# The moving inputs of the products with stationary weights begin 448 bytes past a multiple of 512, the weights' parts on one

## The chip, the cores and the metric

The kernel runs on one core of a Trainium2 chip, in one launch. The metric is the device time of that launch in microseconds (us). The engines are TensorE (PE in the rows, its weight loads PEld), VectorE (DVE), ScalarE (ACT), GpSimd (POOL) and SyncE (SP, which here issues the loads of the weights).

## The reference

Two layers of a streaming encoder on 256 tokens of width 2048, all in float32. Layer 0 mixes tokens by differential attention, layer 1 by an RWKV-7 recurrence; a squared-ReLU MLP of width 8192 follows each.

```python
def sqrelu_mlp(h, w1, w2):
    u = jax.nn.relu(h @ w1)
    return (u * u) @ w2

def reference(x, ...):
    for i in range(DEPTH):            # 2
        hn = rms_norm(x, g_pre_mix[i])
        if i % N_MIXERS == 0:
            m = diff_attention(hn, da_wq[j], da_wk[j], da_wv[j], da_wo[j], ...)
        else:
            m = rwkv7_time_mix(hn, rw_mix[j], rw_wr[j], rw_wk[j], rw_wv[j], rw_wo[j], ...)
        x = x + rms_norm(m, g_post_mix[i])
        hn = rms_norm(x, g_pre_ffn[i])
        x = x + rms_norm(sqrelu_mlp(hn, ffn_w1[i], ffn_w2[i]), g_post_ffn[i])
    return x
```

## The kernel before

Every large product is made of three products in the type float32r: each float32 operand is split in two parts, hi and lo, and hi x hi, lo x hi and hi x lo are added up in PSUM. The weights come from HBM in units of 1 MB (128 partitions x 2048 numbers), as two raw tiles of 512 KB each, issued on SyncE's queue (`raw`, L109). `parts` (L104) splits a raw tile: ScalarE casts it to `whi` (L106), VectorE subtracts to get `wlo` (L107). There are four buffers each of `raw`, `whi` and `wlo`, so two units of each; the next unit is fetched while the one before is multiplied.

There are two forms of the product. In `mm_b` (L217, with `mm_bh`, L225) the weights are stationary: a 128 x 128 block of `whi` or `wlo` is loaded into the array and 256 columns (all tokens) of the input move past it. A unit is 48 such matmuls, 2 column blocks x 8 chunks of the contraction x 3:

```python
            xh, xl = XH[c][:, k, :], XL[c][:, k, :]
            nc.tensor.matmul(ps[m], lhsT=wh[:, k, cl], rhs=xh, start=first and k == 0, stop=False)
            nc.tensor.matmul(ps[m], lhsT=wh[:, k, cl], rhs=xl, start=False, stop=False)
            e = nc.tensor.matmul(ps[m], lhsT=wl[:, k, cl], rhs=xh, start=False, stop=last and k == 3)
```

It serves the query and key projections, the first product of both MLPs, and the r and k projections of RWKV. In `mm_a` (L199) it is the other way round: 128 tokens of the input are stationary and 512 columns of the weights move, 24 matmuls to a unit. It serves the value and output projections and the second product of the MLPs. Plain float32 products, not split, are in the attention scores, in the LoRA panels of RWKV (L752) and in its scan.

The inputs of `mm_b` are the tiles `xh`, `xl` of attention (L404, L405), `fxh`, `fxl` of the MLPs (L577, L578), each 4 chunks x 256 tokens, 4,096 bytes per partition, and `mh`, `ml` of RWKV (L735), of the same size, from a pool that is opened behind the constants' tile `rcst` (L698) and the tiles R. ScalarE and VectorE write them (`gained`, L274, and `split`, L690).

By the sizes of what is allocated ahead of them, all of these begin on a multiple of 512 bytes in each partition: `whi` at 35,328 = 69 x 512 and three times 4,096 above, `wlo` at 51,712 = 101 x 512 and above, `xh0` at 110,592 = 216 x 512, `fxh0` at 107,520 = 210 x 512, the first of `mh` at 98,816 = 193 x 512. A chunk of an input is 1,024 bytes and a block of weights 512, so every operand of every float32r product begins on a multiple of 512.

The order of the work is the program's on each engine. `proj_b` (L236) goes through panels of 256 outputs, two units each, and evacuates PSUM behind each panel; side jobs (`beside`, `tick`) are put between half units, in RWKV above all.

Of the kernel before, what the change touches and what calls it, by code (L numbers as in the profile page):

```python
# [10 lines left out]
F32 = mybir.dt.float32  # L11
F32R = mybir.dt.float32r
# [7 lines left out]
S = 256  # L20
P = 128
# [13 lines left out]
class Kern:  # L35
# [38 lines left out]

    def ps(self, role):
        return self.pp.tile([P, 512], F32, name="ps_" + role, tag=role, bufs=self.roles[role])

    def small(self, n, name):
        return self.sm.tile([P, n], F32, name=name, tag="sm", bufs=48)
# [118 lines left out]

    def mm_a(self, ps, XH, XL, unit, kt0, first, last, ts=range(2), x=slice(0, 512)):  # L199

        nc = self.nc
        for t in ts:
            for half in range(2):
                wh, wl = (w.rearrange("p (k c) -> p k c", k=2)[:, :, x] for w in unit[half])
                for k in range(2):
                    kt = kt0 + half * 2 + k
                    xh = XH[kt // 4][:, kt % 4, t * P:(t + 1) * P]
                    xl = XL[kt // 4][:, kt % 4, t * P:(t + 1) * P]
                    st = first and half == 0 and k == 0
                    sp = last and half == 1 and k == 1  # L210
                    nc.tensor.matmul(ps[t][:, x], lhsT=xh, rhs=wh[:, k, :], start=st, stop=False)  # L211
                    nc.tensor.matmul(ps[t][:, x], lhsT=xh, rhs=wl[:, k, :], start=False, stop=False)  # L212
                    e = nc.tensor.matmul(ps[t][:, x], lhsT=xl, rhs=wh[:, k, :], start=False, stop=sp)  # L213
                self.tick()
        return e

    def mm_b(self, ps, XH, XL, unit, kt0, first, last):  # L217

        for m in range(2):
            for half in range(2):  # L220
                e = self.mm_bh(ps, XH, XL, unit[half], kt0 // 4 + half, m, first and half == 0, last and half == 1)
                self.tick()
        return e

    def mm_bh(self, ps, XH, XL, half, c, m, first, last, ks=range(4)):  # L225
        nc = self.nc
        wh, wl = (w.rearrange("p (k c) -> p k c", k=4) for w in half)
        cl = slice(m * P, (m + 1) * P)
        for k in ks:
# [4 lines that stand above are left out]
        return e  # L234
# [153 lines left out]
    def attention(self, xs):  # L388
        nc, a, tc = self.nc, self.a, self.tc
        with ExitStack() as ctx:  # L390
# [3 lines left out]
            xhl = ctx.enter_context(tc.tile_pool(name="at_x", bufs=1))  # L394
# [3 lines left out]
            XH, XL = [], []  # L398
# [2 lines left out]
            ps0 = [pb[:, S * m:S * m + S] for m in range(2)]  # L401
            loads = []
            for c in range(4):
                XH.append(xhl.tile([P, 4, S], F32R, name=f"xh{c}"))  # L404
                XL.append(xhl.tile([P, 4, S], F32R, name=f"xl{c}"))  # L405
                raw = self.wp.tile([P, 1024], F32, name="raw", tag="raw", bufs=RAW)
                for k in range(0, 4, 2):
                    x = slice(k * 256, (k + 2) * 256)
                    nc.sync.dma_start(raw[:, x], a["wq"][0, c // 2][:, 1024 * (c % 2):1024 * (c % 2) + 1024][:, x])
                    nc.sync.dma_start(xt[c][:, k:k + 2, :], a["xT"][c][:, k:k + 2, :])  # L410
                loads.append(raw)
# [9 lines left out]
            cst = ac.tile([P, 768], F32, name="cst")  # L421
# [147 lines left out]
    def ffn(self, i, xs, fin, store=None):  # L569
# [3 lines left out]
        with ExitStack() as ctx:  # L573
            pool = ctx.enter_context(tc.tile_pool(name=f"ff{i}", bufs=8))
            tmp = ctx.enter_context(tc.tile_pool(name=f"ff{i}_t", bufs=2))
            xhl = ctx.enter_context(tc.tile_pool(name=f"ff{i}_x", bufs=1))
            XH = [xhl.tile([P, 4, S], F32R, name=f"fxh{c}") for c in range(4)]  # L577
            XL = [xhl.tile([P, 4, S], F32R, name=f"fxl{c}") for c in range(4)]  # L578
            gf = self.vec[f"gf{i}"]

            ps0 = [self.ps(r)[:, :S] for r in ("mm", "mm", "a", "a")]
# [88 lines left out]
    def rwkv(self, xs, fin, xctx, pctx):  # L670
        nc, a, tc = self.nc, self.a, self.tc
        outer = ExitStack()
        pool = outer.enter_context(tc.tile_pool(name="rw", bufs=1))
# [21 lines left out]
        with ExitStack() as kc:  # L695
            rp = kc.enter_context(tc.tile_pool(name="rr", bufs=1))

            cst = rp.tile([P, 896], F32, name="rcst")  # L698
            nc.gpsimd.dma_start(cst[:, :776], a["c_rw"][:, P:])
            self.restart = cst[:, 0:512]  # L700
            self.ind = cst[:, 512:520].rearrange("p (i h) -> p i h", i=2)
# [4 lines left out]
            with ExitStack() as ctx:  # L706
# [81 lines left out]
                for c in range(4):  # L788
# [3 lines left out]
                    for k0 in range(0, 4, step):  # L792
# [9 lines left out]
                        f = nc.scalar.copy(MH[c][:, kk, :], m[:, kk, :])  # L802
# [692 lines left out]
```

## Time and profile before

| | |
|---|---|
| median of 3 runs | 2516.78 us (2514.69 to 2521.74) |
| the profiled execution | 2519.97 us, span 2518.2 us |
| PE busy | 2468.2 us, 98% |
| PE weight loads busy | 2245.1 us, 89% |
| VectorE busy | 1596.0 us, 63% |
| ScalarE busy | 1161.5 us, 46% |
| GpSimd busy | 207.2 us, 8% |
| HBM read and written | 433.99 and 15.20 MB, 178 GB/s over the span |
| mean granted TensorE clock | 0.992 of full speed |

A matmul's busy time runs from its start to a modelled end and overlaps the next one's, so how fast PE goes is read from the distances between starts. PEld is the loading of stationary blocks, which runs beside the matmuls.

### The profile page before, as it was taken

The page shows a single profiled execution, that of the slowest core. Times are in us where ns is not written, and L with a number is a line of the kernel's source. Part 1 is how long each engine was busy: PE and PEld are TensorE (multiplying, and loading weights), DVE is VectorE, ACT ScalarE, POOL GpSimd, SP SyncE. Part 2 cuts the span into 40 slices and gives each one's busy share as a digit, 9 for nine tenths or more (in the row PEclk, how much of TensorE's full clock was granted, in tenths as well). Part 3 has the DMA queues.
Part 4 walks back from the last instruction along what each step waited for, and adds up shares of the span by engine and source line. Part 5 has one row for each costly group of instructions (what it writes and reads, how often), then busy time and mean ns, then how long its engine had stood idle before and what let it go on. Part 6 is the DMA issues. An engine that isn't in the chain of part 4 may idle for free.

```text
span 2518.2 us, 42348 instructions
## 1 busy us (share of the span) xinstructions
PE 2468.2 (98%) x17128; PEld 2245.1 (89%) x17128; DVE 1596.0 (63%) x2498; ACT 1161.5 (46%) x1669; POOL 207.2 (8%) x234
## 2 busy tenths in 40 slices
PE   8999999999999999997999999999999999999997
PEld 8998889989989989986899988888998998998986
DVE  6667978645655556669578865557864555654655
ACT  5435645444434434455555543444544444443443
POOL 1000000000000000014301252211000000000001
PEclk9999999999999999998999999999999999999999
DMA  8655455555555555553456764334555555555554
GB/s 279 200 188 178 150 168 170 186 196 186 184 195 188 186 190 185 189 183 124 157 171 217 250 197 129 99 93 165 173 186 191 187 186 193 184 186 195 186 190 138
DMA packets 140852, 453.01 MB, mean 180 GB/s; under 512 B 27536, under 2 KB 27792, under 8 KB 140656
## 3 DMA queue, kind: packets, MB, share of 16 engines
q1 hardware_dynamic: 120176, 424.46, 51.3%
q0 software_dynamic: 5568, 16.52, 1.8%
q10 hardware_dynamic: 14912, 9.32, 1.2%
q8 instruction: 134, 2.20, 0.4%
q14 instruction: 62, 0.51, 0.1%
HBM read 433.99 MB, written 15.20 MB: 178 GB/s over the span
## 4 chain that ended last, share of the span: by engine, by line
PE 93%; DVE 4%; issue 1%; ACT 1%; POOL 0%; DMA 0%; SPq 0%; DVEq 0%; ACTq 0%
PE ps_mm L231 8%; PE ps_mm L232 8%; PE ps_mm L233 8%; PE ps_mm L211 7%; PE ps_mm L213 7%; PE ps_mm L212 7%; PE ps_a L211 7%; PE ps_a L233 6%; PE ps_a L232 6%; PE ps_a L231 6%; PE ps_a L212 6%; PE ps_a L213 6%; PE ps_c L1165 1%; DVE wlo L107 1%; PE ps_mm L1250 1%
## 5 line engine op out<-in xcount | busy, mean ns | idle before, releaser
L107 DVE TENSOR_TENSOR wlo<-raw,whi 128x1024 fp32r<-128x1024 f32 (+1 forms) x766 | 937.8, 1228 | 632.6 <-ACT whi L106 617.6
L106 ACT CAST whi<-raw 128x1024 fp32r<-128x1024 f32 (+1 forms) x776 | 809.0, 1046 | 703.2 <-PE ps_mm L213 221.3
L231 PE MATMUL ps_mm<-fxh,whi 128*128 128x256 f32 x1024 | 290.2, 284 | 0.0
L232 PE MATMUL ps_mm<-fxl,whi 128*128 128x256 f32 x1024 | 290.0, 283 | 0.0
L231 PE MATMUL ps_a<-fxh,whi 128*128 128x256 f32 x1024 | 289.8, 283 | 0.0
L232 PE MATMUL ps_a<-fxl,whi 128*128 128x256 f32 x1024 | 289.8, 283 | 0.0
L233 PE MATMUL ps_a<-fxh,wlo 128*128 128x256 f32 x1024 | 289.8, 283 | 0.0
L233 PE MATMUL ps_mm<-fxh,wlo 128*128 128x256 f32 x1024 | 289.7, 283 | 0.0
L211 PE MATMUL ps_mm<-whi,uh 128*128 128x512 f32 (+1 forms) x544 | 208.3, 383 | 0.0
L212 PE MATMUL ps_mm<-wlo,uh 128*128 128x512 f32 (+1 forms) x544 | 208.3, 383 | 0.0
L213 PE MATMUL ps_mm<-whi,ul 128*128 128x512 f32 (+1 forms) x544 | 208.2, 383 | 0.0
L232 PEld LDWEIGHTS ps_mm<-fxl,whi 128*128 128x128 f32 x1024 | 196.5, 192 | 0.3
L231 PEld LDWEIGHTS ps_a<-fxh,whi 128*128 128x128 f32 x1024 | 196.6, 192 | 0.0
L232 PEld LDWEIGHTS ps_a<-fxl,whi 128*128 128x128 f32 x1024 | 196.6, 192 | 0.0
L233 PEld LDWEIGHTS ps_a<-fxh,wlo 128*128 128x128 f32 x1024 | 196.6, 192 | 0.0
L231 PEld LDWEIGHTS ps_mm<-fxh,whi 128*128 128x128 f32 x1024 | 196.3, 192 | 0.3
L233 PEld LDWEIGHTS ps_mm<-fxh,wlo 128*128 128x128 f32 x1024 | 196.5, 192 | 0.0
L212 PE MATMUL ps_a<-wlo,uh 128*128 128x512 f32 (+1 forms) x512 | 196.0, 383 | 0.0
L213 PE MATMUL ps_a<-whi,ul 128*128 128x512 f32 (+1 forms) x512 | 195.7, 382 | 0.0
L211 PE MATMUL ps_a<-whi,uh 128*128 128x512 f32 (+1 forms) x512 | 195.5, 382 | 0.0
L628 ACT CAST uh<-r 128x256 fp32r<-128x256 f32 x128 | 51.8, 406 | 272.7 <-DVE r L627 272.7
L232 PE MATMUL ps_mm<-ml,whi 128*128 128x256 f32 x416 | 119.5, 288 | 6.5 <-DVE ml L803 6.5
(404 smaller groups left out, 4816.5 us busy)
## 6 DMA issues: line engine op xcount, KB each, us to landing
raw<-in_ffn SPq DMA_DIRECT2D x512, 512.0 KB, 4.3
raw<-in_wk SPq DMA_DIRECT2D x32, 512.0 KB, 4.3
raw<-in_wv SPq DMA_DIRECT2D x32, 512.0 KB, 4.3
raw<-in_wo SPq DMA_DIRECT2D x32, 512.0 KB, 4.2
raw<-in_rwr SPq DMA_DIRECT2D x32, 512.0 KB, 4.6
raw<-in_rwk SPq DMA_DIRECT2D x32, 512.0 KB, 4.3
raw<-in_rwv SPq DMA_DIRECT2D x32, 512.0 KB, 4.9
raw<-in_rwo SPq DMA_DIRECT2D x32, 512.0 KB, 4.2
```

The lines of the kernel that those rows point to most:

```text
L106: self.nc.scalar.copy(hi[:, x], src[:, x])
L107: (eng or self.nc.vector).tensor_tensor(lo[:, x], src[:, x], hi[:, x].bitcast(F32), op=ALU.subtract)
L211: nc.tensor.matmul(ps[t][:, x], lhsT=xh, rhs=wh[:, k, :], start=st, stop=False)
L212: nc.tensor.matmul(ps[t][:, x], lhsT=xh, rhs=wl[:, k, :], start=False, stop=False)
L213: e = nc.tensor.matmul(ps[t][:, x], lhsT=xl, rhs=wh[:, k, :], start=False, stop=sp)
L231: nc.tensor.matmul(ps[m], lhsT=wh[:, k, cl], rhs=xh, start=first and k == 0, stop=False)
L232: nc.tensor.matmul(ps[m], lhsT=wh[:, k, cl], rhs=xl, start=False, stop=False)
L233: e = nc.tensor.matmul(ps[m], lhsT=wl[:, k, cl], rhs=xh, start=False, stop=last and k == 3)
L628: nc.scalar.copy(UH[-1][:, m % 4, :], r)
L1165: nc.tensor.matmul(ps[:, c, :], lhsT=KB[q][x, i, c, :], rhs=AR[q][x, i, c].rearrange("p s t -> p (s t)"), start=True, stop=True)
L1250: nc.tensor.matmul(wps[c][:, h * 64:(h + 1) * 64], lhsT=QT[h][bK(c):bK(c) + 64, c, 0:64], rhs=VU[bK(c):bK(c) + 64, c, h * 64:(h + 1) * 64] ...
```

## The change

A helper makes a tile of 1,152 numbers instead of 1,024 and hands out the 1,024 that begin 448 bytes in. The input tiles of attention and of the MLPs come from it. In RWKV the constants' tile is made 64 bytes shorter (880 numbers instead of 896), and everything that is allocated behind it on that side begins 64 bytes lower, which is 448 past a multiple of 512: the tiles `hw`, `ha`, R, the pool with `mh` and `ml`, and the work tiles of the scan operands. The weights' parts stay where they were, and so do the inputs of the value and output projections of RWKV, those of attention's output projection, and those of the second product of the MLPs. The value projection of attention uses `xh` and `xl` too, as stationary blocks.

The padding keeps each tile's size a multiple of 512 (4,608 bytes), so `fxh1` begins 4,608 behind `fxh0`, and what comes behind the padded tiles stays on a multiple of 512.

```diff
+    def shifted(self, pool, name, o=448):
+
+        t = pool.tile([P, 1024 + 128], F32R, name=name)
+        return t[:, o // 4:o // 4 + 1024].rearrange("p (k t) -> p k t", k=4)
...
-                XH.append(xhl.tile([P, 4, S], F32R, name=f"xh{c}"))
-                XL.append(xhl.tile([P, 4, S], F32R, name=f"xl{c}"))
+                XH.append(self.shifted(xhl, f"xh{c}"))
+                XL.append(self.shifted(xhl, f"xl{c}"))
...
-            XH = [xhl.tile([P, 4, S], F32R, name=f"fxh{c}") for c in range(4)]
-            XL = [xhl.tile([P, 4, S], F32R, name=f"fxl{c}") for c in range(4)]
+            XH, XL = ([self.shifted(xhl, f"fx{y}{c}") for c in range(4)] for y in "hl")
...
-            cst = rp.tile([P, 896], F32, name="rcst")
+            cst = rp.tile([P, 880], F32, name="rcst")
```

## Rows read from the trace of the kernel before

**Rows 1.** The page: busy us, share of the span; the chain that ended last.
```profile
PE 2468.2 (98%) x17128; PEld 2245.1 (89%) x17128; DVE 1596.0 (63%) x2498; ACT 1161.5 (46%) x1669; POOL 207.2 (8%) x234
...
PE 93%; DVE 4%; issue 1%; ACT 1%; POOL 0%; DMA 0%; SPq 0%; DVEq 0%; ACTq 0%
```

**Rows 2.** Matmuls of line L231: duration ns min/median/max, first and last start.
```profile
L231 PE MATMUL ps_mm<-fxh,whi x1024: 277/283/366, 406.4 to 2403.7; 128*128 128x256 f32 x171
L231 PE MATMUL ps_a<-fxh,whi x1024: 283/283/283, 419.9 to 2415.2; 128*128 128x256 f32 x171
L231 PE MATMUL ps_mm<-mh,whi x416: 274/283/467, 1150.3 to 1420.3; 128*128 128x256 f32 x139
L231 PE MATMUL ps_mm<-xh,whi x256: 279/283/584, 6.5 to 183.6; 128*128 128x256 f32 x128
L231 PE MATMUL ps_a<-xh,whi x256: 279/283/388, 21.1 to 195.1; 128*128 128x256 f32 x128
L231 PE MATMUL ps_a<-mh,whi x96: 278/283/468, 1216.2 to 1291.6; 128*128 128x256 f32 x96
```

**Rows 3.** Timeline, first product of the MLP: start us, us, what.
```profile
600.11 0.28 PE L231 MATMUL ps_a<-fxh,whi 128*128 128x256 f32 x1
600.11 0.19 PEld L232 LDWEIGHTS ps_a<-fxl,whi 128*128 128x128 f32 x1
...
601.19 0.28 PE L231 MATMUL ps_a<-fxh,whi 128*128 128x256 f32 x1
```

**Rows 4.** Stretches: PE, PEld, DVE, ACT, POOL busy (count), clock, DMA share, GB/s.
```profile
21.00:195.00 174.00, 173.47 (x1442) 172.86 (x1441) 107.33 (x127) 74.36 (x95) 6.82 (x14) 1.00 0.66 209
587.90:679.90 92.00, 92.00 (x768) 92.00 (x767) 56.44 (x78) 40.17 (x48) 0.00 (x0) 1.00 0.56 184
680.00:766.90 86.90, 86.90 (x386) 71.97 (x385) 44.30 (x42) 34.08 (x33) 0.00 (x0) 1.00 0.58 193
1168.90:1173.70 4.80, 0.50 (x2) 0.30 (x2) 4.80 (x8) 2.18 (x3) 0.99 (x2) 1.00 0.59 234
1174.00:1177.00 3.00, 2.99 (x14) 2.99 (x15) 3.00 (x4) 1.71 (x4) 3.00 (x1) 0.50 0.90 232
1302.00:1420.00 118.00, 118.00 (x1073) 117.00 (x1072) 103.04 (x227) 72.60 (x139) 18.55 (x32) 1.00 0.64 211
```

**Rows 5.** Timeline, second product of the MLP, 512 columns, steady.
```profile
700.00 0.39 PE L212 MATMUL ps_mm<-wlo,uh 128*128 128x512 f32 x1
...
701.36 0.39 PE L212 MATMUL ps_mm<-wlo,uh 128*128 128x512 f32 x1
```

**Rows 6.** Timeline, the 256-column product at a granted clock of 0.50.
```profile
1175.03 0.41 PE L233 MATMUL ps_mm<-mh,wlo 128*128 128x256 f32 x1
...
1176.31 0.41 PE L233 MATMUL ps_mm<-mh,wlo 128*128 128x256 f32 x1
```

**Rows 7.** Timeline, a LoRA panel in plain float32: 13 matmuls merged.
```profile
1259.20 2.97 PE L752 MATMUL ps_b<-m,raw 128*128 128x256 f32 x13
```

**Rows 8.** Timeline, the 256-column product right behind a LoRA panel.
```profile
1262.12 0.28 PE L232 MATMUL ps_mm<-ml,whi 128*128 128x256 f32 x1
...
1262.83 0.28 PE L232 MATMUL ps_mm<-ml,whi 128*128 128x256 f32 x1
```

**Rows 9.** Timeline, switch from the 512-column to the 256-column product.
```profile
587.88 0.28 PE L231 MATMUL ps_mm<-fxh,whi 128*128 128x256 f32 x1
587.99 0.28 PE L232 MATMUL ps_mm<-fxl,whi 128*128 128x256 f32 x1
```

**Rows 10.** Timeline, switch from the 256-column to the 512-column product.
```profile
500.81 0.40 PE L211 MATMUL ps_mm<-whi,uh 128*128 128x512 f32 x1
...
502.20 0.39 PE L211 MATMUL ps_mm<-whi,uh 128*128 128x512 f32 x1
```

**Rows 11.** ScalarE's split, L106: idle us before it, times, and until what.
```profile
  PE ps_mm L232: 139.4, 132
```

**Rows 12.** Waits of PE: us in total, times, longest us.
```profile
PE ps_mm L231 <- ACT xh L276: 6.5, 1, 6.5
```

## Prediction

> **What bounds the kernel now.** I began with the page's busy times and its chain: the matrix engine (PE) is busy 98% of the span and carries 93% of the chain that ended last, while VectorE stands at 63% and ScalarE at 46% [rows 1]. So an edit pays if it changes how fast products start. A busy time of PE does not tell that, because a matmul's 283 ns overlaps the next one's; the start-to-start distance, which I call the pitch, does, and the timeline shows it.
>
> The instructions of one source line give the counts. The 256-column product with stationary weights is written at L231 to L233, and L231 alone has 1024 + 1024 + 416 + 256 + 256 + 96 = 3,072 matmuls [rows 2]; L232 and L233 have as many, in all 9,216. In the timeline of a steady stretch the product that starts at 600.11 and the one that starts at 601.19 us are nine apart: 1.08 / 9 = 120.0 ns [rows 3]. The table of stretches agrees: 768 in 92.00 us [rows 4]. So these products hold 9,216 x 0.120 = 1,106 us, 44% of the span; all are touched by the change.
>
> At the full clock 256 columns at 2.4 GHz are 106.7 ns; 13.3 ns of each pitch is something else. Three rows narrow down what.
> - The product with 512 columns (L211 to L213) has six pitches in 1.36 us, 226.7 ns each [rows 5]. Its columns are 213.3 ns, so it too has 13.3 ns on top: the excess comes once per product, not per column.
> - At 1168.9 to 1173.7 us PE was busy for 0.50 of 4.80 us, waiting, and then the granted clock is 0.50 of full speed, 1.2 GHz, for 3 us [rows 4]. There the 256-column product has six pitches in 1.28 us, 213.3 ns [rows 6], which is 256 / 1.2 to the tenth: no excess at all. So it is not a number of the array's own clock ticks.
> - The plain float32 product of the LoRA panels, also 256 columns, takes two ticks per column: 12 pitches in 2.97 - 0.38 us, 216 ns against 213.3 [rows 7], an excess of 2.5 ns.
>
> The excess shows where the moving operand is read at one column per 2.4 GHz tick, and nearly vanishes where it is read half as fast. What happens once per product, whatever its columns, is the weight load, and the timeline has it at the same time as a moving read: the LDWEIGHTS for the next product starts at 600.11 us with the matmul of the one before [rows 3]. Both reads begin on a multiple of 512 bytes today, by the addresses in the section on the kernel, and the weights of one product are 128 x 4 = 512 bytes per partition. My theory is that the two reads meet in the same place of SBUF and the faster one loses 13.3 ns.
>
> **The change part by part.** *Instructions.* No instruction, DMA or wait is added, removed or reordered. The new tiles are 512 bytes longer, which costs room only; the constants' tile is loaded by the same 776-column DMA. At nothing I cost also the writes of the shifted tiles by ScalarE and VectorE: they stay on a multiple of 64 bytes. If that were wrong, the place to pay is the stretch of the scan operands, where VectorE is busy 103 of 118 us [rows 4] and could absorb 15 us.
>
> *The 9,216 products.* Their moving slice now begins 448 bytes past a multiple of 512 and the weights do not, so the two reads no longer start in the same place. Lower bound of the new pitch: the excess of the float32 product, 106.7 + 2.5 = 109.2 ns. Upper bound of a gain: six pitches behind a change of work, where the weight load's position against the stream differs slightly, take 0.71 us, 118 ns [rows 8]. In between, the first pitch after a switch from 512 to 256 columns is 0.11 us, 105 to 115 ns as the view rounds [rows 9], and the two MLPs have six such switches; it is the shortest pitch of this product at full clock that I found to recur. Upper bound of a loss: after the switch from 256 to 512 columns six pitches of the 512-column product take 1.39 us, 232 ns, 5 ns more than it settles at [rows 10]; so the excess can also grow with the phase, here from 13.3 to 18.4. I take 113 ns, between the two bounds of a gain and inside what the 0.11 us row allows: the stall mostly goes. Some 200 of the 9,216 run at half clock or directly behind a wait (an estimate from the stretches before the first 21 us and from 1150 to 1300 us) and gain nothing: 9,000 x 7 ns = 63 us. The ends: 9,000 x 10.8 = 97 us gained at 109.2; 9,000 x 2 = 18 us gained at 118; 9,216 x 5 = 46 us lost at 125.
>
> On what the memory allows, the Trainium skill speaks against this change: its page "SBUF — State Buffer", section "Who interferes with whom", gives PE two independent read ports, one for the moving operand and one for LDWEIGHTS, and says that PE never waits on anyone. By that rule no shift can matter, the pitch stays at 120 ns and the sum is zero. The trace neither confirms nor refutes it, as every pair of operands in these products has the same distance. The page "TensorE: Matmul & The Clock Gate", section "Wait — 56ns, not 53.3ns?", gives a warm pitch of columns / 2.4 plus about 2.5 ns; this trace's 120 ns for 256 columns is 10.8 ns over it, and by it the sum would be the 97 us of the lower bound.
>
> *The products in which the shifted tile is the weight.* The value projection of attention reads xh and xl as weights against the weight panels at a multiple of 512: 3 x 128 products of 512 columns. Their distance changes too. Between losing 10.8 and gaining 5 ns each, it is 4 us down to 2 us up; I take zero. The other 512-column products have both operands where they were.
>
> *What comes late next.* At 113 ns a weight unit (48 products) lasts 5.42 us instead of 5.76; at 109.2 it lasts 5.24. The 1 MB of a unit then asks for 193 to 200 GB/s, where the first projections already run at 209 and the 512-column stretch at 193 [rows 4]. The splits are behind PE, not ahead of it: ScalarE's cast stands idle 139.4 us until these products free a buffer [rows 11], and VectorE is busy 56.44 of 92.00 us in the stretch [rows 4], which would be 56.44 of 86.8. No wait of PE on a split or an input sums to more than 6.5 us in the whole span; one of that size is the first of all, on attention's input [rows 12]. So the gain reaches the end.
>
> *The sum.* The profiled execution took 2,519.97 us; less 63 that is 2,457. The median of the runs is 3.2 us lower, 2,516.8, and less 63 it is 2,454 us.
>
> **The rivals.**
> 1. *The excess is fixed* and belongs to switching weights for this data type; addresses play no part. For it: 226.7 and 120.0 have the same 13.3 ns to the tenth, although the four weight buffers and the chunks give many different places; none of these pairs differs in its distance within 512 bytes, though. Against it: the 0.11 us and the 232 ns [rows 9, 10], which a fixed cost does not give. Time: 2,517 us, within 0.3% (7.6 us; about what a measurement here can tell from no change). The skill's rule of two ports, cited above, is this case.
> 2. *The shift makes it worse.* The moving read now begins in the last 64 bytes of a 512-byte stretch and touches three such stretches, not two; if the two reads meet again later in the stream, where the weight load is still under way, the excess grows as in the 232 ns row. It decides from a pitch of 120.8 ns up (9,216 x 0.8 = 7.6 us). At 125 ns: 2,563 us.
> 3. *The products get faster and the feed takes the place.* At 109.2 ns the raw tiles would have to land at 200 GB/s. Against it: 209 in the first projections. Only the 118 us with the scan operands look tight (VectorE 103): 768 products x 10.8 = 8.3 us could shrink to nothing there, so even then 2,428 us, faster.
>
> **How the numbers follow.** Forecast, pitch 109 to 118 (rival 3 included): 0.60, at 2,420 to 2,499 us by itself. Fixed excess: 0.25. Worse: 0.15. The forecast has the fast and slow phases of the trace and the vanishing at half speed behind it; the fixed cost has the identical 13.3 ns; the loss has the 232 ns row alone. A point of 2,454. The range reaches from all of the excess but 2.5 ns gone, with a few us for the value projection (2,417), through no change up to a slight loss (2,526): 0.57 of the forecast, 0.25, and a little of the loss. Chances: faster 0.60, same 0.25, slower 0.15.
>
> **What would show it.** In the timeline of the changed kernel the pitch at L231 to L233 in a steady stretch is 113 (109 to 118) instead of 120.0, the 92.0 us stretch is 86.8, L211 to L213 in the MLP keep 226.7, and 213.3 at half clock stays. ScalarE's idle time behind these products falls by about as much as the span. A pitch of exactly 120.0 makes rival 1 right; over 121, rival 2; a shorter pitch with new waits of PE for wlo or whi, rival 3.

## The result and the profile after

The kernel after takes 2,489.15 us (median of 4 runs, 2,489.04 to 2,493.24); the kernel before, on the same chip, 2,518.72 (4 runs, 2,514.69 to 2,521.74). The ratio is 0.9888, interval 0.9869 to 0.9906: 29.6 us, or 1.1%, faster. I had said 2,454, a gain of 63 us, with a range of 2,417 to 2,526. The sign came out as forecast; the size is less than half of it.

The profiled execution took 2,493.24 us with a span of 2,491.5, which is 26.7 us less than before. The page's busy times and its chain (compare [rows 1]; the line numbers are 5 higher now, so L231 to L233 are L236 to L238):

```profile
PE 2437.7 (98%) x17128; PEld 2214.8 (89%) x17128; DVE 1595.8 (64%) x2498; ACT 1161.6 (47%) x1669; POOL 205.6 (8%) x234
...
PE 92%; DVE 4%; issue 1%; DMA 1%; ACT 1%; POOL 0%; SPq 0%; DVEq 0%; ACTq 0%
```

The same instructions run; what changed is the distance between matmul starts. The timeline of the kernel after shows the 256-column product twice, once in attention (from 159.81 us) and once in the MLP (from 600.09 us):

```profile
159.81 0.28 PE L238 MATMUL ps_a<-xh,wlo 128*128 128x256 f32 x1
...
161.17 0.28 PE L238 MATMUL ps_a<-xh,wlo 128*128 128x256 f32 x1
...
600.09 0.28 PE L236 MATMUL ps_a<-fxh,whi 128*128 128x256 f32 x1
...
601.15 0.28 PE L236 MATMUL ps_a<-fxh,whi 128*128 128x256 f32 x1
```

The attention pair is twelve products apart: 1.36 / 12 = 113.3 ns. The MLP pair is nine apart: 1.06 / 9 = 117.8 ns. Before, it was 120.0 in both [rows 3]. So the same instruction, with the same start distance between its operands and no wait ahead of it, now has two paces. I call them the quick and the slow rhythm. Counting starts in 80 us finds them quickly. Expect 669 at 120.0 ns (667, and two that began ahead of the stretch), 681 or 682 at 117.8, and 708 at 113.3. Stretches of the kernel after, columns as in [rows 4]:

```profile
100.00:180.00 80.00, 80.00 (x708) 80.00 (x708) 51.20 (x54) 31.84 (x31) 3.85 (x8) 1.00 0.61 198
425.00:485.00 60.00, 60.00 (x511) 59.89 (x510) 41.45 (x65) 26.49 (x35) 0.00 (x0) 1.00 0.56 188
525.00:575.00 50.00, 50.00 (x223) 41.40 (x222) 23.05 (x19) 22.13 (x23) 0.00 (x0) 1.00 0.57 191
585.00:665.00 80.00, 80.00 (x682) 80.00 (x681) 51.07 (x71) 35.92 (x43) 0.00 (x0) 1.00 0.57 189
1790.00:1850.00 60.00, 59.98 (x527) 59.62 (x527) 42.91 (x68) 28.20 (x37) 0.00 (x0) 1.00 0.61 200
1945.00:2025.00 80.00, 80.00 (x682) 80.00 (x681) 50.66 (x70) 34.86 (x42) 0.00 (x0) 1.00 0.57 185
```

The first row is attention, quick. The MLPs' first products come in four groups each. Group 1 of the first MLP is slow here (511 in 60 us), that of the second MLP quick (527). Groups 2 to 4 of both, the fourth and sixth row standing for them, are slow. The third row is the 512-column product: 223 in 50 us, the count that the kernel before has in the same window. Its timeline has six pitches of 226.7 ns, as in [rows 5], and at half clock, where the 1160 to 1163 us stretch has a granted clock of 0.50, six pitches of the 256-column product take 1.28 us as in [rows 6]:

```profile
699.84 0.39 PE L217 MATMUL ps_a<-wlo,uh 128*128 128x512 f32 x1
...
701.20 0.39 PE L217 MATMUL ps_a<-wlo,uh 128*128 128x512 f32 x1
...
1160.77 0.41 PE L236 MATMUL ps_mm<-mh,whi 128*128 128x256 f32 x1
...
1162.05 0.41 PE L236 MATMUL ps_mm<-mh,whi 128*128 128x256 f32 x1
```

Where the time went, from the first start of each stretch to the start of the large product that follows it, in the two timelines:

| stretch | before, us | after, us | change |
|---|---|---|---|
| attention, query and key | 188.98 | 181.71 | -7.3 |
| first MLP, group 1 | 94.43 | 92.46 | -2.0 |
| second MLP, group 1 | 94.43 | 90.14 | -4.3 |
| MLP groups 2 to 4, six stretches | 92.15 each | 90.45 each | -10.2 |
| RWKV, r and k | 272.4 | 270.3 | -2.1 |
| attention, value projection | 105.9 | 106.2 | +0.3 |

These add up to -25.6 of the 26.7 us. Attention would have 1,536 x 6.7 = 10.2 us at the quick rhythm. In the profiled execution it had one wait for a split that the profile before lacks, 2.4 us at 56 us, the third row of the waits of PE in the kernel after (us in total, times, longest). The first is that of [rows 12]; the second had the same sum before. That the shorter pitch caused this wait is not shown: `offsets_d` below, with attention at 120.0 ns, has it too, the last row.

```profile
PE ps_mm L236 <- ACT xh L281: 6.8, 1, 6.8
...
PE ps_a L238 <- DVE wlo L112: 3.8, 2, 3.3
...
PE ps_mm L238 <- DVE wlo L112: 2.4, 1, 2.4
```

```profile
PE ps_mm L238 <- DVE wlo L112: 2.3, 1, 2.3
```

Two questions remain. Is it the distance between the two reads that acts, or the address of one of them? And what makes six of the eight MLP groups gain 2.2 ns and not 6.7? Below, "distance" is the start of the moving operand less the start of the stationary one, modulo 512 bytes.

### The profile page after: what moved, and what is told of

The parts are those of the page before. It is cut to its first block, busy times and chain, and to the rows that moved or that the text cites. A ratio compares the mean times of both kernels' runs of the same rounds, so it can differ in the third digit from the quotient of the medians.

```text
span 2491.5 us, 42348 instructions
## 1 busy us (share of the span) xinstructions
PE 2437.7 (98%) x17128; PEld 2214.8 (89%) x17128; DVE 1595.8 (64%) x2498; ACT 1161.6 (47%) x1669; POOL 205.6 (8%) x234
## 4 chain that ended last, share of the span: by engine, by line
PE 92%; DVE 4%; issue 1%; DMA 1%; ACT 1%; POOL 0%; SPq 0%; DVEq 0%; ACTq 0%
PE ps_mm L236 8%; PE ps_mm L237 7%; PE ps_mm L238 7%; PE ps_mm L218 7%; PE ps_mm L216 7%; PE ps_mm L217 7%; PE ps_a L216 7%; PE ps_a L217 6%; PE ps_a L218 6%; PE ps_a L238 6%; PE ps_a L236 6%; PE ps_a L237 6%; PE ps_c L1169 1%; DVE wlo L112 1%; PE ps_mm L1254 1%
## 5 line engine op out<-in xcount | busy, mean ns | idle before, releaser
L236 PE MATMUL ps_mm<-fxh,whi 128*128 128x256 f32 x1024 | 287.7, 281 | 0.0
L236 PE MATMUL ps_a<-fxh,whi 128*128 128x256 f32 x1024 | 286.9, 280 | 0.0
L238 PE MATMUL ps_a<-fxh,wlo 128*128 128x256 f32 x1024 | 286.9, 280 | 0.0
L238 PE MATMUL ps_mm<-fxh,wlo 128*128 128x256 f32 x1024 | 286.9, 280 | 0.0
L238 PEld LDWEIGHTS ps_a<-fxh,wlo 128*128 128x128 f32 x1024 | 195.9, 191 | 0.0
L238 PEld LDWEIGHTS ps_mm<-fxh,wlo 128*128 128x128 f32 x1024 | 195.9, 191 | 0.0
L236 PEld LDWEIGHTS ps_mm<-fxh,whi 128*128 128x128 f32 x1024 | 192.2, 188 | 0.6 <-DVE r L630 0.2
L236 PEld LDWEIGHTS ps_a<-fxh,whi 128*128 128x128 f32 x1024 | 192.2, 188 | 0.0
```

## The experiments

### Distance or address

Two kernels ran beside the kernel before (2,517.8 us, 13 runs). The first shifts the stationary operands too, so that the distance is zero again while nothing lies on a multiple of 512. The second moves the weights and leaves the inputs.

```diff
 # all_at_448, from the kernel before
-        self.ones = self.cp.tile([P, P], F32, name="ones")
+        self.ones = self.cp.tile([P, P + 112], F32, name="ones")[:, :P]
-            cst = rp.tile([P, 896], F32, name="rcst")
+            cst = rp.tile([P, 784], F32, name="rcst")
 # weights_at_64, from the kernel after
+        self.ones = self.cp.tile([P, P + 16], F32, name="ones")[:, :P]
```

> The kernel before with one constants' tile 448 bytes longer, so that weights' parts and inputs both begin 448 past a multiple of 512 in attention and in both MLPs: the moving operand's own address is that of the changed kernel, its distance from the weights within 512 bytes is 0 as before. In RWKV's r and k projections the inputs come to lie at 0 and the weights at 448, a distance of 64. Theory A (the distance between the two reads counts): 120.0 ns in all MLP and attention stretches of the 256-column product, in all about the time of before, 2519 us, but for RWKV (1,536 products, between 113 and 125 ns, so -10 to +8 us). Theory B (the moving operand's own start counts): 113 to 118 ns there as in the changed kernel, about 2491 us.

> The changed kernel with one constants' tile 64 bytes longer: the weights' parts begin 64 past a multiple of 512 and the inputs of the 256-column products on one; the distance is 448 as in the changed kernel. Theory A (distance): 117.8 ns in the MLP stretches entered from the 512-column product, 113.3 ns in attention, about 2489 us in all. Theory B (the moving operand's own start): 120.0 ns everywhere, about 2519 us.

The first took 2,512.46 us (10 runs), ratio 0.9979 [0.9967, 0.9991]; the second 2,488.75 (4 runs), ratio 0.9896 [0.9877, 0.9915]. Stretches in attention and in the first MLP, first of the one kernel, then of the other:

```profile
100.00:180.00 80.00, 80.00 (x669) 80.00 (x668) 47.56 (x51) 30.01 (x30) 3.84 (x8) 1.00 0.59 190
590.00:670.00 80.00, 80.00 (x669) 80.00 (x668) 49.45 (x69) 34.69 (x41) 0.00 (x0) 1.00 0.57 185
```

```profile
100.00:180.00 80.00, 80.00 (x681) 80.00 (x681) 48.69 (x51) 30.03 (x30) 3.84 (x8) 1.00 0.60 194
590.00:670.00 80.00, 80.00 (x681) 80.00 (x681) 50.47 (x72) 35.12 (x42) 0.00 (x0) 1.00 0.56 188
```

With both operands at 448 the pitch is 120.0 ns again; with the weights at 64 and the inputs back on 512 it is shorter again. So it is the distance. The small gain of the first kernel lies where its distance is not zero: the r and k projections of RWKV, at distance 64, have a mean pitch of 116.5 ns and took 268.0 us, not 272.4 (and not the 270.8 that they take in each of two other kernels with all distances at zero, one_product_unshifted and narrow_weights below). The second kernel shows something more. In the profiled run attention ran quick (223 starts in 25 us) up to a wait of 2.4 us at 56 us and slow (215) behind it, at a distance at which the kernel after ran quick on both sides of such a wait:

```profile
25.00:50.00 25.00, 25.00 (x223) 25.00 (x222) 14.95 (x19) 12.88 (x23) 1.03 (x2) 1.00 0.85 269
75.00:100.00 25.00, 25.00 (x215) 25.00 (x214) 14.49 (x13) 10.21 (x14) 0.96 (x2) 1.00 0.61 196
```

So the distance allows the two rhythms but does not choose between them.

### Which distances

Three kernels give each stretch a distance of its own by changing the argument of `shifted`, and in RWKV the size of `rcst`.

```diff
-                XH.append(self.shifted(xhl, f"xh{c}"))
+                XH.append(self.shifted(xhl, f"xh{c}", 64))
-            XH, XL = ([self.shifted(xhl, f"fx{y}{c}") for c in range(4)] for y in "hl")
+            XH, XL = ([self.shifted(xhl, f"fx{y}{c}", (128, 192)[i]) for c in range(4)] for y in "hl")
```

| kernel | attention | first MLP | RWKV | second MLP | us (1 run each) |
|---|---|---|---|---|---|
| offsets_c | 64 | 128 | 384 | 192 | 2,505.68 (before there: 2,517.8) |
| offsets_d | 256 | 320 | 256 | 384 | 2,510.70 (the same) |
| fine_offsets | 32 | 16 | 480 | 48 | 2,503.66 (before there: 2,520.39) |

> The changed kernel with other distances: 64 in attention, 128 in the first MLP, 384 in RWKV's projections, 192 in the second MLP. If any distance but 0 helps equally, the second to fourth panels' stretches of both MLPs stand at 117.8 ns and attention at 113.3. If only the read that begins one 64-byte block before the weights' (448) is free of the meeting, all stretches stand at 120 ns or more. If the meeting is moved along the stream by the distance, the pitch differs from stretch to stretch between 109 and 125 ns.

> As the run before with 256 in attention, 320 in the first MLP, 256 in RWKV's projections, 384 in the second MLP. Same three answers: 117.8 and 113.3 ns if any distance helps, 120 or more if only 448 does, and values from 109 to 125 ns that change with the distance if the meeting is moved along the stream.

> The changed kernel with distances that are no multiple of 64: 32 in attention, 16 in the first MLP, 480 (-32) in RWKV's projections, 48 in the second MLP. The runs so far gave 120.0 ns at 0, 128, 256 and 384 and 117.8 or 113.3 at 64, 192, 320 and 448, a period of 128 bytes. If two 64-byte halves of a 128-byte line are what the two reads share or miss, 16, 32 and 48 lie between (part of the columns meets): pitches between 113 and 120 that change with the distance. If the rows of memory are finer than 64 bytes, 32 or 16 alone gives 117.8 or less. If only an exact multiple of 64 counts, all stand at 120.0 or above.

In each kernel, the stretches of attention, of the first and of the second MLP (group 2 in both MLPs), offsets_c, then offsets_d, then fine_offsets:

```profile
100.00:180.00 80.00, 80.00 (x682) 80.00 (x681) 48.69 (x51) 29.80 (x30) 3.86 (x8) 1.00 0.59 194
590.00:670.00 80.00, 80.00 (x669) 80.00 (x668) 50.07 (x70) 35.08 (x42) 0.00 (x0) 1.00 0.55 183
1960.00:2040.00 80.00, 80.00 (x682) 80.00 (x681) 50.27 (x70) 35.76 (x43) 0.00 (x0) 1.00 0.57 188
```

```profile
100.00:180.00 80.00, 80.00 (x670) 80.00 (x668) 47.56 (x51) 29.48 (x30) 3.86 (x8) 1.00 0.59 188
590.00:670.00 80.00, 80.00 (x682) 80.00 (x681) 50.76 (x70) 34.88 (x42) 0.00 (x0) 1.00 0.56 186
1960.00:2040.00 80.00, 80.00 (x669) 80.00 (x669) 50.25 (x70) 35.07 (x42) 0.00 (x0) 1.00 0.55 184
```

```profile
100.00:180.00 80.00, 80.00 (x688) 80.00 (x687) 48.61 (x51) 30.72 (x30) 3.84 (x8) 1.00 0.61 195
590.00:670.00 80.00, 80.00 (x676) 80.00 (x675) 50.47 (x71) 35.16 (x42) 0.00 (x0) 1.00 0.57 188
1960.00:2040.00 80.00, 80.00 (x678) 80.00 (x678) 50.70 (x71) 35.07 (x42) 0.00 (x0) 1.00 0.56 186
```

At 64, 192 and 320 the slow rhythm is there (682); at 128, 256 and 384 the mean in these stretches is 120 ns as at zero (669, 670). But 128 and 384 are not quite like zero. Group 1 of the first MLP in offsets_c, at 128, counts 508 in 60 us, where the kernel before counts 502: 118.7 ns.

```profile
435.00:495.00 60.00, 60.00 (x508) 60.00 (x507) 39.48 (x57) 27.55 (x34) 0.00 (x0) 1.00 0.56 182
```

```profile
435.00:495.00 60.00, 60.00 (x502) 60.00 (x502) 38.98 (x60) 27.40 (x35) 0.00 (x0) 1.00 0.56 186
```

Group 1 of the second MLP in offsets_d and RWKV in offsets_c, both at 384, stand at 118.7 as well, and where the mean is 120 at these two distances the single pitches run from 117 to 123; at 0 and 256 every steady one is 120. So odd multiples of 64 bytes help in every stretch, 128 and 384 in some by about 1 ns, 256 not at all: 448 is nothing special, and 512 is not the measure that counts. At 32, 16 and 48 the counts lie between (688, 676 and 678; means of 116.7, 118.7 and 118.3 ns).

### The rhythm is chosen on the way in

Groups 2 to 4 are entered straight from the 512-column product, attention and group 1 are not. In `entry_dummy` a few small float32 products, whose result nobody reads, stand at the head of each of the six groups; their number and width differ from group to group.

```diff
+                n, w = (((0, 0), (1, 128), (2, 128), (4, 128)), ((0, 0), (1, 32), (4, 32), (3, 128)))[i][fb]
+                if n:
+                    side = self.ps("b")
+                for j in range(n):
+                    nc.tensor.matmul(side[:, P * j:P * j + w], lhsT=self.ident, rhs=self.ident[:, :w], start=True, stop=True)
                 self.proj_b(w1, XH, XL, evac, range(fb * 8 + 2 * (fb == 0), fb * 8 + 8), ["mm", "a"])
```

> The changed kernel, with one to four small plain float32 products, of which nothing is read, on PE between the 512-column product and the next panels' 256-column products: 1, 2 and 4 of 128 columns before the panels 2, 3 and 4 of the first MLP, then 1 and 4 of 32 columns and 3 of 128 in the second. Theory: at a distance of 448 the product has two stable rhythms, 113.3 and 117.8 ns, and the way PE enters the stretch picks one. Then some of the six stretches fall from 117.8 to 113.3 ns (-3.4 us each), the others stay. Rival: the rhythm belongs to the stretch itself (its buffers, or the work of ScalarE and VectorE beside it); then all six stay at 117.8 ns and the time grows by about 1 us.

It took 2,475.87 us (1 run; before there 2,520.39). The first and the last of six stretches:

```profile
585.00:665.00 80.00, 80.00 (x708) 80.00 (x707) 51.63 (x72) 36.83 (x44) 0.00 (x0) 1.00 0.60 196
...
2285.00:2365.00 80.00, 80.00 (x708) 80.00 (x708) 51.87 (x72) 35.29 (x43) 0.00 (x0) 1.00 0.58 194
```

All six count 708, whatever the number and width of the small products, where only some were expected to: quick instead of slow for 768 products each, 87.14 us instead of 90.45, for 0.14 to 0.81 us of entry.

`one_product` puts just one such product of 128 columns ahead of each group; `one_product_unshifted` does the same to the kernel before. `every_panel` puts one at the head of every panel (`self.nc.tensor.matmul(ps[0][:, :P], lhsT=self.ident, rhs=self.ident, start=True, stop=True)` in `proj_b`). The kernel before took 2,514.76 us beside these three (7 runs).

> The changed kernel with one plain float32 product of 128 columns, of which nothing is read, ahead of the panels 2, 3 and 4 of each MLP. Theory (the way PE enters the stretch picks the rhythm): all six stretches at 113.3 instead of 117.8 ns, 6 x (3.4 - 0.15) = 19.5 us under the changed kernel's 2489, 2470 us. Rival (the run before had it by luck): a mixture, 2470 to 2490 us.

> The kernel before with the same six products. Theory: at a distance of 0 there is one rhythm, 120.0 ns, however PE enters; 120.0 in all six stretches and about 1 us more than before, 2519 us. Rival (the break alone makes the products faster, and the shift has little to do with it): 113.3 ns in the six stretches, about 2490 us.

> The changed kernel with one such product at the head of every panel of the 256-column product (62 of them, 0.15 us each, 9 us in all), in attention and RWKV too. If each break leads to 113.3 ns, attention (113.5 to 117.6 so far), RWKV (116) and the MLPs stand at 113.3 and the time is 2470 + 8 - up to 10 us, about 2470; if a break can also lead from 113.3 to 117.8, some stretches show both and the time is up to 2490.

| kernel | us | ratio to before |
|---|---|---|
| one_product | 2,470.31 (4 runs, 2,465.53 to 2,475.87) | 0.9817 [0.9797, 0.9838] |
| one_product_unshifted | 2,515.97 (1 run) | |
| every_panel | 2,500.44 (4 runs, 2,498.13 to 2,503.73) | 0.9937 [0.9918, 0.9955] |

Group 2 of the first MLP in one_product, in one_product_unshifted and in every_panel:

```profile
585.00:665.00 80.00, 80.00 (x708) 80.00 (x707) 53.29 (x74) 36.14 (x44) 0.00 (x0) 1.00 0.59 194
```

```profile
590.00:670.00 80.00, 80.00 (x669) 80.00 (x668) 48.55 (x68) 34.60 (x42) 0.00 (x0) 1.00 0.56 184
```

```profile
590.00:670.00 80.00, 80.00 (x695) 80.00 (x694) 50.92 (x71) 35.70 (x43) 0.00 (x0) 1.00 0.57 187
```

At distance zero there is one rhythm only: the small product changes nothing (669). At 448 it brings the quick one (708). In every_panel (695) both occur, in turn from panel to panel, so a break is not good in itself: it can lead from quick to slow as well. The first two panels of this group, 98 starts in 10.8 us and 98 in 11.3:

```profile
584.30:595.10 10.80, 10.80 (x98) 10.80 (x97) 5.93 (x8) 4.98 (x6) 0.00 (x0) 1.00 0.59 195
595.30:606.60 11.30, 11.30 (x98) 11.30 (x97) 7.02 (x11) 4.91 (x6) 0.00 (x0) 1.00 0.54 178
```

every_panel took 10 us more than the 2,490 expected at most. Against the kernel after, groups 2 to 4 stand where they were (90.47 us each: what half of the panels gain, the eight breaks cost again, some 0.2 us each), and attention (+4.9 us) and group 1 of the second MLP (+3.1), which ran quick there, are half slow here. `one_product` beats both kernels, the changed one by 2,489.15 - 2,470.31 = 19 us as far as medians from two chips can be set side by side; by the ratios it is 0.9817 against 0.9888, and their intervals do not meet.

### The 512-column product

If 13.3 ns is lost there too, can a distance win some back? The stationary inputs of the MLPs' second product (`uh`, `ul`) are shifted within a padded tile in the kernel after.

```diff
-                        UH.append(pool.tile([P, 4, S], F32R, name="uh", tag="pan"))
+                        UH.append(self.panel(pool, "uh", (96, 112)[i]))   # u_shift_64: (64, 32)
```

> The changed kernel, and the stationary tiles of the MLPs' 512-column product begin 96 (first MLP) and 112 (second) past a multiple of 512, so the moving weights are at a distance of -96 (32 modulo 128) and -112 (16) from them. If the same meeting of reads sets the 13.3 ns there, the pitch falls from 226.7 to between 216 and 224 ns (up to 3,168 x 7 ns = 22 us). If the 512-column product keeps its place whatever the distance, 226.7. In attention, RWKV and its output projection distances of 64 and 448 made that product slower (229 to 233), so up to 233 can come too, +20 us.

> As the run before, with the stationary tiles 64 past (first MLP, a distance of 448) and 32 past (second MLP, a distance of 480, that is 96 modulo 128). By the other 512-column products at 448, which stood at 233 ns, the first MLP gets 233 instead of 226.7 ns, 1,464 x 6.6 = +10 us; 226.7 if those stood at 233 because of their many interruptions. For the second MLP any value from 216 to 233.

They took 2,504.46 and 2,506.66 us (1 run each; before there 2,520.39), ratios of 0.994 and 0.995 where the kernel after has 0.9888. The 512-column stretch in u_shift_fine (distance 416), then in u_shift_64 (distance 448):

```profile
525.00:575.00 50.00, 50.00 (x215) 40.16 (x215) 21.69 (x18) 21.12 (x22) 0.00 (x0) 1.00 0.55 187
```

```profile
525.00:575.00 50.00, 50.00 (x216) 40.30 (x215) 22.06 (x18) 21.10 (x22) 0.00 (x0) 1.00 0.57 187
```

215 and 216 instead of 223: some 233 ns instead of 226.7, and 400 and 480 in the second MLP gave the same 233. This product loses about 6.7 ns at a distance of 448, where the 256-column one gains. The value and output projections of RWKV in all_at_448, at 448 as well, have a mean of 233.3 ns between neighbouring starts, and 229.2 in the kernel before. Distance 64, in attention's value projection of the kernel after, cost next to nothing (+0.3 us in the table above; 228.9 ns instead of 226.9 in its longest unbroken run of starts).

The two kernels also show something of the entry. Their 256-column products are those of the kernel after, no small product stands ahead of any group, and groups 2 to 4 come straight from the 512-column product, which now runs at another pace. Group 2 of the first and of the second MLP in u_shift_fine:

```profile
585.00:665.00 80.00, 80.00 (x681) 80.00 (x680) 50.19 (x70) 35.74 (x42) 0.00 (x0) 1.00 0.56 185
1960.00:2040.00 80.00, 80.00 (x708) 80.00 (x708) 51.81 (x72) 36.80 (x44) 0.00 (x0) 1.00 0.59 197
```

Here all three groups of the second MLP run quick, and in u_shift_64 three of the six. So it does not take a small product: a changed pace ahead of the group can bring the quick rhythm too.

### Is the loss in proportion to the weights' read?

In the kernel before, groups 2, 3 and 4 of the first MLP load only the first 96, 64 and 32 columns of each weight block, so the weights' read gets shorter and the moving read stays. The outputs of the other columns are left out, so the kernel computes something else.

```diff
-        cl = slice(m * P, (m + 1) * P)
+        cl, o = slice(m * P, m * P + self.cols), ps[m][:self.cols]
-            nc.tensor.matmul(ps[m], lhsT=wh[:, k, cl], rhs=xh, start=first and k == 0, stop=False)
+            nc.tensor.matmul(o, lhsT=wh[:, k, cl], rhs=xh, start=first and k == 0, stop=False)
```

> The kernel before, where the 256-column product of the first MLP's panels 2, 3 and 4 loads only the first 96, 64 and 32 columns of each block of 128 weights and leaves the other outputs out (set to zero). Theory: the excess of 13.3 ns comes from the weights' reads that meet the moving ones and shrinks with them: pitches of 116.7, 113.3 and 110 ns if in proportion to the columns, instead of 120.0. Rival (a fixed cost of switching weights at this distance): 120.0 ns in all three.

It took 2,504.32 us (1 run). The three groups:

```profile
595.00:675.00 80.00, 80.00 (x692) 80.00 (x691) 54.55 (x83) 35.21 (x43) 0.00 (x0) 1.00 0.58 189
770.00:850.00 80.00, 80.00 (x708) 80.00 (x707) 56.34 (x85) 36.04 (x44) 0.00 (x0) 1.00 0.58 194
945.00:1025.00 80.00, 80.00 (x682) 73.28 (x681) 53.85 (x83) 35.57 (x43) 0.00 (x0) 1.00 0.56 186
```

116.0, 113.3 and 117.8 ns, where proportion said 116.7, 113.3 and 110. That the pitch depends on the width of the load at all, at distance zero, rules out a fixed cost per change of weights. The first two widths agree with proportion; the third does not: it shows 682, the count of the slow rhythm. Proportion alone falls with it. A narrower load also leaves fewer outputs to be written, and this run does not tell the two apart.

## Why the prediction was right in its sign and wrong in its size

**What bounds the kernel, and what the excess is.** Right in the first, in part in the second. All but some 1 us of the gain lies in the stretches of the 256-column product, and its pitch answers to the start distance of the moving read and the weights' read (all_at_448 against weights_at_64) and to the width of the weight load (narrow_weights). That the two reads meet in one place of SBUF is a guess that fits this and is not shown; half of the excess answered to no distance, and the 512-column product, with the same 13.3 ns, is at its best at distance zero. Where I spoke of multiples of 512, distances of 128, 256 and 384 bring little more than 1 ns at most. The change picked 448, an odd multiple of 64, without knowing that this counts: that was luck.

**The step that failed: "I take 113 ns", one pitch for 9,000 products.** There are two rhythms, and 113.3 is only one of them. The 4,608 products of the MLPs' groups 2 to 4 ran at 117.8: 4,608 x 2.2 = 10 us, where the sum had 4,608 x 7 = 32; that is 22 of the 36 us that are missing from the 63. I had both numbers, 118 as a bound, but as one pitch to be found between bounds. That both came so near the two rhythms is luck, since neither row showed a pace: the 118 ns behind a LoRA panel [rows 8] is the mean of six uneven pitches, and from 1262.83 us on that product stands at 120 again, as the line below, nine products later, shows. I chose 113 by the first pitch behind a switch from 512 to 256 columns, 0.11 us [rows 9], and the one behind it is 0.12 already.

```profile
1263.91 0.28 PE L232 MATMUL ps_mm<-ml,whi 128*128 128x256 f32 x1
```

The same place in the kernel after, in its timeline, has 0.12 from the first product on, and stays there:

```profile
579.24 0.28 PE L236 MATMUL ps_mm<-fxh,whi 128*128 128x256 f32 x1
579.36 0.28 PE L237 MATMUL ps_mm<-fxl,whi 128*128 128x256 f32 x1
```

So the very switch that made me pick 113 is the one behind which the slow rhythm sets in. entry_dummy and one_product show that it is the way in that decides: a single small product between the two turns 117.8 into 113.3 for the 768 products after it. With it the kernel takes 2,470, most of the way to 2,454.

**The rest of the shortfall.** Attention got its 113.3, less the 2.4 us wait: 7.3 us where the sum had 10.8. Group 1 of the first MLP was slow for most of its length; the two groups 1 brought 6.3 us of 10.8. In RWKV, where waits and side work break the stream, the distances between neighbouring starts at full clock (some 1,400 in each timeline, those of 100 to 135 ns) have a mean of 116.5 ns, before 119.8. That is 1,400 x 3.3 = 4.6 us, not 7 ns each; and only 2.1 us of it arrived. Most of the difference is the clock: 48 such distances were at a granted clock of 0.50 (213 or 214 ns), before 25, and 23 x 0.097 = 2.2 us.

**The lower bound, 109.2 ns.** No 256-column product with full weights settled below 113.3 at any distance tried. The Trainium skill, page "TensorE: Matmul & The Clock Gate", section "Wait — 56ns, not 53.3ns?", gives columns / 2.4 plus about 2.5 ns, which is that 109.2; no float32r product here agrees with it, the nearest being 113.3. Half of the excess, 6.7 ns, stays, and no run here says why.

**Parts at nothing.** Right: VectorE's and ScalarE's busy times are those of before within 0.2 us, so the shifted writes cost nothing; the value projection moved by 0.3 us; the MLP's 226.7 and the 213.3 at half clock stayed.

**What comes late next.** Nearly right. ScalarE's splits wait for buffers less than before [rows 11]. The same group and the next one in the kernel after, and that next one in the kernel before:

```profile
  PE ps_mm L237: 131.5, 133
  PE ps_a L237: 94.0, 121
```

```profile
  PE ps_a L232: 105.5, 122
```

Together that is 19.4 us less, of the 26.7 by which the span fell; I had said about as much as the span. The feed was in time but for the one 2.4 us wait at 56 us, which cannot be put down to the change.

**The rivals.** The first, an excess that is fixed as a whole, falls by all_at_448 with weights_at_64 and again by narrow_weights; the 6.7 ns that answered to no distance may be fixed. The Trainium skill, page "SBUF — State Buffer", section "Who interferes with whom", calls PE's two read ports independent and says that PE never waits on anyone. For this product the trace does not agree with their independence as I had read it: distance alone moves the pitch from 120.0 to 113.3. The second, a loss, did not happen to the 256-column products, but a distance can cost time: u_shift_fine and u_shift_64 show the 512-column product losing 6.7 ns. That a later meeting of the reads is the reason, as I had argued, is not shown. The third, the feed, amounts to 2.4 us at most.

**What stays open.** What the two rhythms are physically, and why a given way in leads to one of them: the runs show that it does, not how. Attention had the quick one in one kernel and mostly the slow one in another at the same distance. one_product's four runs spread over 10 us; their granted clock goes with it, 0.993 in the shortest and 0.989 in the longest, and whether a rhythm caught differently has a share in it is open, as only one of them has a trace. Why 32 weight columns fall into the slow count, why the 512-column product is best at zero, and what the 6.7 ns left are, no run here settles.

## What to carry to other kernels

When the matrix engine is bound by its own products, read the distance between starts in every stretch and set it beside columns over clock; an excess that is the same per product is a reason to try other start distances of the two operands, in steps of 64 bytes, for each product shape by itself, since what helped 256 columns hurt 512. Look for more than one stable pace and for what stands at the head of each stretch; here one product of 128 columns that nobody reads was worth 3 us ahead of a group of 768, and one ahead of every 96 gained nothing over none. A single pitch behind a switch is no forecast of the pace; take it from many starts, far from any break.

## What the hardware showed that I had not expected

- A stream of equal products, with no wait, has two stable rhythms at one and the same distance, 113.3 and 117.8 ns, and keeps the one that it settled in until the next break. At distance zero there is one, 120.0 ns.
- The pitch depends on the distance in steps far finer than 512 bytes: 113.3 or 117.8 ns at the odd multiples of 64 tried, 120.0 at 0 and 256, 120 or 118.7 at 128 and 384, and 116.7 to 118.7 at 16, 32 and 48.
- The sign depends on the shape: at 448 the 256-column product gains up to 6.7 ns, the 512-column product loses about as much (226.7 to 233).
- A narrower weight load shortens the pitch of a product whose moving side is unchanged: 96 columns 116.0 ns, 64 columns 113.3, but 32 columns 117.8.
